# Layer-0 attention: the head norm's Newton steps on GpSimd, and the last 16 keys split on GpSimd from SBUF

## The chip, the cores and the metric

One Trainium2 chip, one core of it. The metric is device time in microseconds of one execution, the median of several runs. The profile is one further execution of the same program, with its own time. TensorE does matmuls and transposes, VectorE, ScalarE and GpSimd work on vectors; TensorE writes to PSUM, and GpSimd works from SBUF alone in this kernel.

## The reference, cut to what matters

An encoder of two layers over 1,040 positions (16 learned meta tokens and 1,024 tokens), width 1,024, all in float32. Layer 0 has two groups of heads. Group A is differential attention: four heads, each with two score maps that share one value matrix, and a norm over the head's output.

```python
def _diff_attention(q, k, v, lam, table, pos):
        ...
        s = jnp.einsum('bqhcd,bshcd->bhcqs', qb, k).astype(jnp.float32) * scale + bias[None, :, None]
        p = jax.nn.softmax(s, axis=-1)
        attn = p[:, :, 0] - lam * p[:, :, 1]
        return jnp.einsum('bhqs,bshv->bqhv', attn.astype(v.dtype), v)
...
    oa = _rmsnorm(oa, subln) * (1.0 - lam_init)
```

Group B is grouped-query attention (eight query heads, two key heads). Then come an output projection, a squared-ReLU MLP, and layer 1 with windowed attention and its own MLP.

## The kernel before

Each float32 operand of a product is split into a high part in the matmul's reduced format and a low part, the difference. A product is two or three matmuls over these parts. An attention weight is therefore transposed on TensorE into PSUM, copied to the high part by ScalarE (L570), and subtracted to the low part by VectorE (L572).

Part A, `head_a` (L603), runs over four heads. For each tile of 128 queries `scores` (L510) makes two maps in three chunks of 346 or 348 keys: matmuls (L519), eviction with the bias and a running minimum by VectorE (L521), the minimum of the three (L531), and the exponential with its row sum by ScalarE (L533). GpSimd then combines the two maps: it multiplies the second by its weight (L642) and adds it to the first (L643). The weight is the first map's sum times minus lambda, over the second map's sum: VectorE takes the reciprocal (L640), GpSimd the product (L641). The first map's own sum is not divided out, since the norm that follows removes it; the norm's epsilon is scaled by its square instead (L659).

Part B, `attend_b` (L685), runs over two key heads and four query heads of each, two query tiles at a time, and twice over the 16 remaining queries. It is the same with one map: VectorE evicts (L524), GpSimd divides (L694).

`pv` (L540) multiplies by the values. It is a generator. A group has two query tiles (in part A also one of two tiles and the 16 remaining queries). For each run of key blocks it transposes, splits and multiplies (L553, L570, L572, L584). The 1,040 keys are eight blocks of 128 and 16 more. For these 16 it transposes keys 912 to 1,039, takes the last 32 rows, and stacks them in one tile `tail`: high, low, and in part A high again, in steps of 32 partitions, against a value block laid out to match. Before the change this is the last step of the generator: ScalarE copies out of PSUM (L596), VectorE subtracts (L594), and the closing matmul (L597) follows. There are 16 such groups in part A and 34 in part B.

The generators wait in a list, `late`. After each group's scores the oldest is run, so that three stay open. The order of the instructions on each engine's queue is set by the framework's scheduler, which simulates the program with a cost table of its own. So the values of one group stand between the scores of later ones. Every queue runs in its order.

The head norm is `norm_a` (L654): ScalarE squares the head's output (L657), `colsum` (L181) sums it over partitions with 18 small matmuls (L187), evicts the sums (L197, L200) and calls `rsqrt_small` (L152). That one starts from a bit trick (L157, L158) and makes three Newton steps of three VectorE operations each (L160 to L162) on 128x9 elements. `norm_b`, placed behind up to two more groups, spreads the result over the partitions with another 18 matmuls (L210), and VectorE multiplies (L663). `rsqrt_small` also serves the other norms of the kernel.

Of the kernel before, what the change touches and what calls it, by code (L numbers as in the profile page):

```python
# [12 lines left out]
F32 = mybir.dt.float32  # L13
# [3 lines left out]
ALU = mybir.AluOpType  # L17
# [4 lines left out]
P = 128  # L22
L = 1040
# [4 lines left out]
EPS = 1e-6  # L28
# [40 lines left out]
def f32(ap):  # L69
    return ap.bitcast(F32)  # L70


def trunk(tc, hT, gT, w_in0, w_out0, w_up, w_down, w_in1, w_out1, rel, sinks, lamv, subln, qkn,
          onehot, ident_d, cos_d, sin_d, out, dbg=None, stop=None):
    nc = tc.nc
    V, A, G, T, D = nc.vector, nc.scalar, nc.gpsimd, nc.tensor, nc.sync
# [75 lines left out]
    def rsqrt_small(x, pw, n):  # L152

        y = sm.tile([P, 24], F32, tag="rs_y", bufs=2, name=nm("rsy"))
        t = sm.tile([P, 24], F32, tag="rs_t", bufs=2, name=nm("rst"))
        yv, tv = y[:pw, :n], t[:pw, :n]
        V.tensor_scalar(tv.bitcast(I32), x.bitcast(I32), 1, None, op0=ALU.arith_shift_right)  # L157
        V.tensor_scalar(yv.bitcast(I32), tv.bitcast(I32), -1, 0x5F3759DF, op0=ALU.mult, op1=ALU.add)  # L158
        for _ in range(3):
            V.tensor_tensor(tv, yv, yv, op=ALU.mult)  # L160
            V.scalar_tensor_tensor(tv, tv, -0.5, x, op0=ALU.mult, op1=ALU.mult)
            V.scalar_tensor_tensor(yv, tv, 1.5, yv, op0=ALU.add, op1=ALU.mult)  # L162
        return y
# [17 lines left out]
    def colsum(acc, c0, n, ps, scale, eps=None):  # L181
# [19 lines left out]
        return rsqrt_small(x[:, :nt], P, nt), tiles  # L201
# [338 lines left out]
    def pv(ps_o, ptiles, vmats, passes, lo_pool=()):  # L540
# [34 lines left out]
        slow = {r: split(r) for r in lo_pool}  # L575
        order = [r for r in range(len(runs)) if r not in slow] + list(lo_pool)
# [11 lines left out]
        pt, _ = transposed([L - P])  # L588
        tl = tails[tail_at[0] % 3]
        tail_at[0] += 1  # L590
        for x, (v, lo) in enumerate(passes):
            rows = slice(32 * x, 32 * x + 32)
            if lo:
                V.tensor_tensor(tl[rows, :gw], pt[96:128, :gw], f32(tl[0:32, :gw]), op=ALU.subtract)  # L594
            else:
                A.copy(tl[rows, :gw], pt[96:128, :gw])  # L596
# [6 lines left out]
    def head_a(h):  # L603
# [18 lines left out]
        for grp in GRPS:  # L622
            ptiles = []
            for t in grp:
# [16 lines left out]
                G.tensor_tensor(b[:, 1:2], es[:, t, 0:1], nlam, op=ALU.mult)  # L641
                G.tensor_scalar(st[1], st[1], b[:, 0:1], b[:, 1:2], op0=ALU.mult, op1=ALU.mult)  # L642
# [11 lines left out]
        def norm_a():  # L654
# [4 lines left out]
            V.scalar_tensor_tensor(e0, es[:, :, 0], EPS, es[:, :, 0], op0=ALU.mult, op1=ALU.mult)  # L659
            y, tiles = colsum(osq, 0, L, bank("tr"), 1.0 / 128, e0)  # L660
# [725 lines left out]
```

## Time and profile before

| | |
|---|---|
| median of 3 runs | 2,571.01 us (2,569.41 to 2,578.85) |
| profiled execution, its own time | 2,573.7 us |
| its span, first to last instruction | 2,571.9 us |
| mean granted clock of TensorE | 0.977 |
| TensorE, VectorE, ScalarE, GpSimd busy | 95%, 76%, 49%, 50% |

A row of the profile names line, engine, operation, what is written and read, and shapes. PE is TensorE's matmuls, PEld its weight loads, DVE VectorE, ACT ScalarE, POOL GpSimd, SP the queue that issues transfers. A busy TensorE isn't one at its peak: matmuls overlap, and the granted clock (1.00 is 2.4 GHz, 0.5 is 1.2 GHz) says how fast it ran. A wait is put down to the event that came last.

### The profile page before, as it was taken

To read this page: it belongs to the slowest core of one execution; us is meant where nothing else is said; L and a number is where in the kernel's file an instruction comes from. 1 tells how busy PE (TensorE), PEld (TensorE's weight loads), DVE (VectorE), ACT (ScalarE), POOL (GpSimd) and SP (SyncE) were. 2 spreads that over 40 slices of the span, in tenths; PEclk is the share of its full clock that TensorE was granted. 3 is DMA by queue.
4 is the path that set the end of the run, shared out by engine and by line. 5 is a ranking of instruction groups with operands and counts; after the bars stand their busy time and mean duration, and the time that the engine had idled before them with its cause. 6 is when DMAs were issued, how large, how long until landed. Compare 5 with 4: busy or idle time off the path is not lost. (4 is left out here: it accounts for less than half of the span.)

```text
span 2571.9 us, 43032 instructions
## 1 busy us (share of the span) xinstructions
PE 2448.4 (95%) x15375; PEld 2224.7 (86%) x15375; DVE 1947.2 (76%) x4059; ACT 1266.1 (49%) x2587; POOL 1283.1 (50%) x1221
## 2 busy tenths in 40 slices
PE   7999999999998999999999999998989999899997
PEld 7999888999998988989999998887878888677776
DVE  7843998899767677779898767787586665889975
ACT  3322766688634333354333447887344444443424
POOL 3300766233155555445666345556365664566645
PEclk9999998999998999999999999999989999999998
DMA  4287534100221733353433342232304334554411
GB/s 134 95 270 243 148 97 121 26 12 12 97 96 64 216 126 125 138 199 124 154 120 113 106 139 69 70 82 70 124 31 165 136 144 142 187 171 131 148 60 72
DMA packets 134614, 307.16 MB, mean 119 GB/s; under 512 B 18656, under 2 KB 49792, under 8 KB 133888
## 3 DMA queue, kind: packets, MB, share of 16 engines
q1 hardware_dynamic: 134400, 304.42, 36.3%
q8 instruction: 121, 1.98, 0.3%
q14 instruction: 93, 0.76, 0.1%
HBM read 214.43 MB, written 98.43 MB: 122 GB/s over the span
## 5 line engine op out<-in xcount | busy, mean ns | idle before, releaser
L876 PE MATMUL st<-h,wh 128*128 128x260 f32 (+1 forms) x2520 | 808.2, 325 | 41.1 <-DVE up L907 16.5
L876 PE MATMUL st<-l,wh 128*128 128x260 f32 (+1 forms) x2520 | 808.5, 323 | 7.7 <-DVE l L801 4.2
L876 PE MATMUL st<-h,wl 128*128 128x260 f32 (+1 forms) x2520 | 778.9, 323 | 6.0 <-DVE wl L133 4.0
L876 PEld LDWEIGHTS st<-h,wh 128*128 128x128 f32 x2520 | 478.1, 191 | 92.6 <-ACT up L908 15.4
L876 PEld LDWEIGHTS st<-l,wh 128*128 128x128 f32 x2520 | 480.7, 191 | 47.1 <-DVE l L996 5.2
L876 PEld LDWEIGHTS st<-h,wl 128*128 128x128 f32 x2520 | 472.6, 191 | 48.6 <-DVE wl L133 5.8
L132 ACT CAST wh<-wr 128x512 fp32r<-128x512 f32 x378 | 232.7, 617 | 420.4 <-PE st L876 197.9
L133 DVE TENSOR_TENSOR wl<-wr,wh 128x512 fp32r<-128x512 f32 x254 | 226.8, 897 | 159.5 <-ACT wh L132 159.0
L133 POOL TENSOR_TENSOR wl<-wr,wh 128x512 fp32r<-128x512 f32 x124 | 171.1, 1379 | 153.6 <-ACT wh L132 146.8
L908 ACT ACTIVATE up<-up 128x260 f32<-128x260 f32 (+1 forms) x192 | 93.5, 491 | 209.6 <-DVE up L907 209.2
L519 PE MATMUL sc<-stk,stk 128*128 128x346 f32 (+1 forms) x768 | 182.1, 353 | 11.8 <-DVE mx L521 11.6
L533 ACT ACTIVATE sp<-sp,mn 128x1040 f32<-128x1040 f32 x134 | 156.4, 1167 | 42.9 <-DVE mn L531 38.1
L996 DVE TENSOR_TENSOR l<-l,h 128x520 fp32r<-128x520 f32 (+1 forms) x182 | 172.7, 951 | 1.8 <-ACT h L994 1.8
L1027 DVE TENSOR_TENSOR h<-h,st 128x260 f32<-128x260 f32 x392 | 150.7, 415 | 28.1 <-PE st L876 26.5
L1027 DVE TENSOR_TENSOR hall<-hall,st 128x512 f32<-128x512 f32 x196 | 131.1, 679 | 28.3 <-PE st L876 27.0
L149 PE MATMUL mm<-l,wh 128*128 128x346 f32 (+3 forms) x440 | 151.1, 343 | 0.3 <-DVE l L784 0.3
L149 PE MATMUL mm<-h,wl 128*128 128x346 f32 (+3 forms) x440 | 149.9, 343 | 0.0
L886 POOL TENSOR_TENSOR ws<-wr 128x512 f32<-128x512 f32 x32 | 43.0, 1344 | 213.9 <-DMA wr<-w_up 191.4
L149 PE MATMUL mm<-h,wh 128*128 128x346 f32 (+3 forms) x440 | 148.3, 343 | 0.6 <-ACT h L783 0.6
L694 POOL TENSOR_SCALAR sp<-sp,rsum 128x1040 f32<-128x1040 f32 x66 | 75.4, 1155 | 144.9 <-DVE rsum L537 56.1
L907 DVE SCALAR_TENSOR_TENSOR up<-up,acc 128x260 f32<-128x260 f32 (+1 forms) x144 | 143.2, 997 | 5.5 <-ACT acc L219 2.1
L132 ACT CAST wh<-ws 128x512 fp32r<-128x512 f32 x120 | 74.3, 619 | 145.1 <-PE st L876 114.9
(286 smaller groups left out, 5980.1 us busy)
## 6 DMA issues: line engine op xcount, KB each, us to landing
wr<-w_down SPq DMA_DIRECT2D x68, 512.0 KB, 4.1
wr<-w_up SPq DMA_DIRECT2D x64, 512.0 KB, 4.1
l<-sd SPq DMA_DIRECT2D x42, 520.0 KB, 5.4
l<-sd SPq DMA_DIRECT2D x42, 512.0 KB, 4.9
stk<-stk_d SPq DMA_DIRECT2D x72, 260.0 KB, 6.5
sd<-up SPq DMA_DIRECT2D x30, 520.0 KB, 2.6
sd<-up SPq DMA_DIRECT2D x30, 512.0 KB, 2.6
wr<-w_in SPq DMA_DIRECT2D x27, 512.0 KB, 6.1
```

The lines of the kernel that those rows point to most:

```text
L132: A.copy(h, src)
L133: lo_on.tensor_tensor(l, src, f32(h), op=ALU.subtract)
L149: T.matmul(ps[:, :n], a[:, k % 4 * P:(k % 4 + 1) * P], x[k][:, o:o + n], start=(k == 0 and i == 0), stop=(k == len(xh) - 1 and i == 2))
L519: T.matmul(ps[:M, :n], q, k[:, o:o + n], start=(i == 0), stop=(i == len(ops) - 1))
L533: A.activation(s[:M, :L], s[:M, :L], AF.Exp, bias=mn[:M, x:x + 1], scale=-1.0, accum_out=sums[:M, x:x + 1])
L694: G.tensor_scalar(s, s, rs[:, i:i + 1], 1.0, op0=ALU.mult, op1=ALU.mult)
L876: T.matmul(acc_[x, o][:, :n], a[:, c], b[:, o:o + n], start=first and k == 0 and y == 0, stop=k == nk - 1 and y == 2, skip_group_check=not ...
L886: G.tensor_tensor(s1, a21, a22, op=ALU.add)
L907: V.scalar_tensor_tensor(r[:, c], src, 0.0, r_[:, c], op0=ALU.max, op1=ALU.mult)
L908: A.activation(r[:, c], r[:, c], AF.Square)
L996: V.tensor_tensor(l, src, f32(h), op=ALU.subtract)
L1027: marks.append(V.tensor_tensor(ht[m][:, c], ht[m][:, c], acc_[x, o][:, :n], op=ALU.add).ins)
```

## The change

Three edits, all in layer-0 attention.

1. In the head norm the three Newton steps run on GpSimd, as four operations each instead of three. The bit trick stays on VectorE. The scaled epsilon is made on GpSimd with two operations instead of one on VectorE. All other norms keep their code.
2. In `pv` the last keys are transposed first in the generator instead of last. ScalarE copies the 32 rows once into a new SBUF tile `traw` (two buffers), and GpSimd makes the parts of `tail` from it. The closing matmul stays last.
3. The weight of the second map is made by one VectorE operation behind the reciprocal, instead of one on GpSimd; the multiplication on GpSimd takes that one scalar.

```diff
-    def rsqrt_small(x, pw, n):
+    def rsqrt_small(x, pw, n, on=V):
...
         for _ in range(3):
-            V.tensor_tensor(tv, yv, yv, op=ALU.mult)
-            V.scalar_tensor_tensor(tv, tv, -0.5, x, op0=ALU.mult, op1=ALU.mult)
-            V.scalar_tensor_tensor(yv, tv, 1.5, yv, op0=ALU.add, op1=ALU.mult)
+            on.tensor_tensor(tv, yv, yv, op=ALU.mult)
+            if on is V:
+                V.scalar_tensor_tensor(tv, tv, -0.5, x, op0=ALU.mult, op1=ALU.mult)
+                V.scalar_tensor_tensor(yv, tv, 1.5, yv, op0=ALU.add, op1=ALU.mult)
+            else:
+                on.tensor_tensor(tv, tv, x, op=ALU.mult)
+                on.tensor_scalar(tv, tv, -0.5, 1.5, op0=ALU.mult, op1=ALU.add)
+                on.tensor_tensor(yv, yv, tv, op=ALU.mult)
...
         slow = {r: split(r) for r in lo_pool}
+        pt, _ = transposed([L - P])
+        tl = tails[tail_at[0] % 3]
+        tail_at[0] += 1
+        raw = getA("traw", [32, 272], F32, 2)
+        A.copy(raw[:, :gw], pt[96:128, :gw])
+        for x, (v, lo) in enumerate(passes):
+            rows = slice(32 * x, 32 * x + 32)
+            if lo:
+                G.tensor_tensor(tl[rows, :gw], raw[:, :gw], f32(tl[0:32, :gw]), op=ALU.subtract)
+            else:
+                G.tensor_copy(tl[rows, :gw], raw[:, :gw])
...
         yield
-        pt, _ = transposed([L - P])
-        tl = tails[tail_at[0] % 3]
-        tail_at[0] += 1
-        for x, (v, lo) in enumerate(passes):
-            rows = slice(32 * x, 32 * x + 32)
-            if lo:
-                V.tensor_tensor(tl[rows, :gw], pt[96:128, :gw], f32(tl[0:32, :gw]), op=ALU.subtract)
-            else:
-                A.copy(tl[rows, :gw], pt[96:128, :gw])
         T.matmul(ps_o[:, :gw], vmats[0][:, 8, :], tl[:, :gw], start=False, stop=True)
...
                 V.reciprocal(b[:, 0:1], es[:, t, 1:2])
-                G.tensor_tensor(b[:, 1:2], es[:, t, 0:1], nlam, op=ALU.mult)
-                G.tensor_scalar(st[1], st[1], b[:, 0:1], b[:, 1:2], op0=ALU.mult, op1=ALU.mult)
+                V.tensor_scalar(b[:, 1:2], b[:, 0:1], es[:, t, 0:1], nlam, op0=ALU.mult, op1=ALU.mult)
+                G.tensor_scalar(st[1], st[1], b[:, 1:2], 1.0, op0=ALU.mult, op1=ALU.mult)
...
-            V.scalar_tensor_tensor(e0, es[:, :, 0], EPS, es[:, :, 0], op0=ALU.mult, op1=ALU.mult)
-            y, tiles = colsum(osq, 0, L, bank("tr"), 1.0 / 128, e0)
+            G.tensor_scalar(e0, es[:, :, 0], EPS, 1.0, op0=ALU.mult, op1=ALU.mult)
+            G.tensor_tensor(e0, e0, es[:, :, 0], op=ALU.mult)
+            y, tiles = colsum(osq, 0, L, bank("tr"), 1.0 / 128, e0, G)
```

`colsum` hands its new argument `on` to `rsqrt_small`.

## Rows read from the trace of the kernel before

**Rows 1.** The page: span; busy time, share and instructions of each engine.

```profile
span 2571.9 us, 43032 instructions
...
PE 2448.4 (95%) x15375; PEld 2224.7 (86%) x15375; DVE 1947.2 (76%) x4059; ACT 1266.1 (49%) x2587; POOL 1283.1 (50%) x1221
```

**Rows 2.** Stretches: length; engines busy (instructions); granted clock; DMA share; GB/s.

```profile
316.00:331.00 15.00, 12.54 (x80) 11.41 (x80) 13.61 (x43) 7.79 (x15) 9.15 (x9) 0.89 0.00 1
331.00:367.00 36.00, 35.50 (x271) 34.50 (x269) 32.60 (x126) 28.28 (x58) 24.21 (x20) 1.00 0.64 167
367.00:391.00 24.00, 19.19 (x99) 15.60 (x98) 22.24 (x73) 11.61 (x22) 16.46 (x15) 0.86 0.26 60
425.00:442.00 17.00, 14.28 (x80) 12.74 (x80) 14.55 (x54) 8.20 (x16) 6.99 (x9) 0.80 0.17 42
477.00:492.00 15.00, 13.11 (x74) 12.50 (x75) 8.86 (x32) 5.15 (x11) 4.03 (x4) 0.66 0.01 2
500.00:660.00 160.00, 158.27 (x1210) 151.76 (x1209) 157.16 (x541) 136.50 (x258) 57.50 (x51) 1.00 0.05 12
255.00:450.00 195.00, 179.33 (x1199) 165.54 (x1198) 174.10 (x659) 133.62 (x264) 129.70 (x110) 0.94 0.45 121
```

**Rows 3.** Waits, 255 to 450 us: who for whom, us, times, longest.

```profile
PEld sc L519 <- DVE mx L521: 18.5, 27, 2.2
POOL sp L642 <- DVE mn L531: 15.9, 4, 5.0
...
PE sc L519 <- DVE mx L521: 11.6, 13, 1.9
```

**Rows 4.** Groups of VectorE, 255 to 495 us: busy us, mean ns; idle before.

```profile
L160 DVE TENSOR_TENSOR rst<-rsy 128x9 f32<-128x9 f32 x12 | 9.8, 818 | 0.2
L594 DVE TENSOR_TENSOR tail<-tr,tail 32x256 fp32r<-32x256 f32 (+2 forms) x17 | 7.2, 423 | 0.5
...
L659 DVE SCALAR_TENSOR_TENSOR e<-es 128x8 f32<-128x8 f32 x4 | 5.4, 1356 | 0.0
L640 DVE RECIPROCAL beta<-es 128x1 f32<-128x1 f32 x32 | 5.0, 157 | 2.7 <-ACT sp L533 2.7
...
L161 DVE SCALAR_TENSOR_TENSOR rst<-rst,cs 128x9 f32<-128x9 f32 x12 | 4.7, 390 | 0.0
...
L157 DVE TENSOR_SCALAR rst<-cs 128x9 int32<-128x9 int32 x4 | 2.5, 626 | 0.1
```

**Rows 5.** Timeline, first head's norm: start us, us, operation, [idle before].

```profile
317.25 2.42 POOL L643 TENSOR_TENSOR sp<-sp,sp 128x1040 f32<-128x1040 f32 x1
317.42 2.28 DVE L160 TENSOR_TENSOR rst<-rsy 128x9 f32<-128x9 f32 x1
...
320.19 0.59 PE L519 MATMUL sc<-stk,stk 128*128 128x348 f32 x2 [1.56 <-DVE mx L521]
```

**Rows 6.** Timeline, second head's norm.

```profile
367.52 2.43 POOL L643 TENSOR_TENSOR sp<-sp,sp 128x1040 f32<-128x1040 f32 x1
...
368.75 1.23 DVE L157 TENSOR_SCALAR rst<-cs 128x9 int32<-128x9 int32 x1
```

**Rows 7.** Groups of GpSimd, 255 to 450 us.

```profile
L642 POOL TENSOR_SCALAR sp<-sp,beta 128x1040 f32<-128x1040 f32 x32 | 39.0, 1220 | 43.9 <-DVE beta L640 25.1 <-DVE mn L531 15.9 <-PE sc L519 2.0
L641 POOL TENSOR_TENSOR beta<-es,nlam 128x1 f32<-128x1 f32 x32 | 6.2, 195 | 13.0 <-ACT sp L533 13.0
```

**Rows 8.** Line 649, ending a differential group: ns min/median/max, first and last start.

```profile
L649 ACT COPY oT<-pv x16: 352/372/393, 284.0 to 474.4; 128x256 f32<-128x256 f32 x12, 128x272 f32<-128x272 f32 x4
```

**Rows 9.** Groups of GpSimd behind layer-0 attention, 700 us to the end.

```profile
L1240 POOL TENSOR_SCALAR s<-s,rsum 128x400 f32<-128x400 f32 (+1 forms) x128 | 76.1, 608 | 43.3 <-DVE rsum L1238 42.3
...
L1269 POOL TENSOR_TENSOR oc<-oc,ob 64x256 f32<-64x256 f32 x40 | 29.7, 744 | 34.5 <-ACT oc L1268 33.0 <-issue 1.2
```

**Rows 10.** Groups, 500 to 660 us.

```profile
L584 PEld LDWEIGHTS pv<-plo,v 128*128 128x128 f32 x207 | 38.9, 188 | 8.0 <-DVE plo L572 6.1 <-DVE mn L531 0.7
...
L594 DVE TENSOR_TENSOR tail<-tr,tail 32x256 fp32r<-32x256 f32 (+1 forms) x26 | 11.0, 422 | 0.8
```

More of the change, by code (lines that the diff above doesn't have):

```diff
@@ L179, in sq_acc, with colsum @@
             add_on.tensor_tensor(acc[:, o:o + n], acc[:, o:o + n], t[:, :n], op=ALU.add)
-    def colsum(acc, c0, n, ps, scale, eps=None):
+    def colsum(acc, c0, n, ps, scale, eps=None, on=V):
         tiles = tok_tiles(c0, n)
@@ L200, in colsum @@
             V.tensor_scalar(x[:w, full:nt], src[:w, full:nt, 0], scale, EPS, op0=ALU.mult, op1=ALU.add)
-        return rsqrt_small(x[:, :nt], P, nt), tiles
+        return rsqrt_small(x[:, :nt], P, nt, on), tiles
     def bcast_cols(y, tiles, newps, use):
```

## The prediction

> **What bounds the kernel now.** I read the page first: TensorE is busy 95% of the span, VectorE 76%, GpSimd 50% [rows 1]. An average over unlike stages says little about an edit confined to one, so next comes the table of stretches of layer-0 attention. It has two parts. From 255 to about 450 us run the four differential heads (part A), from 500 to 700 the grouped-query heads (part B). In part A VectorE is busy 174.1 of 195 us, GpSimd 129.7 [rows 2]; in the steady stretch of part B VectorE is busy 157.2 of 160 us [rows 2]. VectorE is the engine to relieve in both.
>
> Four short stretches stand out: 316 to 331, 367 to 391, 425 to 442 and 477 to 492 us. They hold 80, 99, 80 and 74 matmuls, 333 in 71 us, or 4.7 per us, while the quiet stretch 331 to 367 holds 271 in 36 us, or 7.5 per us. The granted clock in them is 0.89, 0.86, 0.80 and 0.66 against 1.00 [rows 2]: part of the time TensorE ran at 1.2 instead of 2.4 GHz. Those four stretches are where the head norm of each of the four heads runs. The waits say who holds TensorE up: scores wait for VectorE's eviction (L521), 18.5 us at the weight loads and 11.6 us at the matmuls, 30.1 us in part A [rows 3].
>
> The group table of VectorE says why it is late. The Newton multiply of the reciprocal root (L160) works on 128x9 elements and takes 818 ns in the mean, the next one (L161; L162 has the same count, time and mean) 390, the small product for the epsilon (L659, 128x8) 1,356, the shift (L157) 626. A reciprocal on 128x1 (L640) takes 157 [rows 4]. The timeline shows the mechanism: GpSimd's add L643 starts at 317.25 and lasts 2.42 us; L160 starts at 317.42 and lasts 2.28, so both end at about 319.7. TensorE's next scores then start after an idle 1.56 us, put down to the eviction queued behind L160 [rows 5]. In the second norm the shift L157, started at 368.75, ends at 369.98 together with the L643 that ran from 367.52 [rows 6]. A tiny VectorE operation here waits out a whole GpSimd operation, and everything in VectorE's queue stands behind it. By the Trainium skill (SBUF — State Buffer, "Who interferes with whom") a VectorE instruction with two SBUF inputs cannot run beside a GpSimd instruction that reads SBUF, and one that has a single SBUF input and is in no two-port mode can; the pairs of rows agree, and so does L640, which never grew.
>
> **The change, part by part.**
>
> *Newton steps and epsilon product leave VectorE.* Per head nine Newton operations and L659 go. They held VectorE 9.8 + 4.7 + 4.7 + 5.4 = 24.6 us [rows 4]. At 157 ns each the forty would take 6.3 us, so 18.3 us of it is waiting for GpSimd. The shift and the subtraction that starts the guess stay, so the shift's waiting (2.5 us less 4 x 0.157, so 1.9) can stay too. What is this worth on the path? Lower bound 0: the column sums and the broadcast matmuls of the norm stay where they were and could keep the clock down by themselves. Upper bound: if all 333 matmuls of the four stretches ran at the quiet rate they would need 333 / 7.53 = 44.2 us, a gain of 26.8. I take 60%, 16 us, because the 18.3 us of waiting is the part with a known cause and because the first stretch shows the stall, not the norm's matmuls, ahead of the slow matmuls.
>
> On GpSimd the same work is twelve Newton and two epsilon operations per head, 56 in all. The nearest row is GpSimd's 128x1 multiply L641, 195 ns [rows 7]: 56 x 0.195 = 10.9 us of GpSimd time. The broadcast that needs the result is issued behind two more groups' values, and one group takes (474.4 - 284.0) / 15 = 12.7 us [rows 8], against 12 x 0.195 = 2.3 us plus at most two pairs of L642 and L643, 1.22 and 2.43 us each [rows 6, 7], 7.3 us. I take its delay at nothing; without that cover, a chain late by one L643 would cost 2.4 us a head, 10 us.
>
> *The last 16 keys' rows.* For each of 50 groups (16 in part A, 34 in part B) VectorE's subtraction L594 goes, 423 ns [rows 4]. ScalarE takes one copy out of PSUM instead of two (A) or one (B). GpSimd gets a subtraction and one or two copies of 32x256. Its nearest rows: a two-input operation on 64x256 takes 744 ns, a one-input one on 128x400 608 [rows 9]. For the copy, which no row shows at this width, the ends are 195 and 744 ns; between L641 and the 400-column row a line gives about 0.45 us, which I take. So 1.19 us a group in part B (40 us, with GpSimd busy 57.5 of 160 in its steady stretch [rows 2]) and 1.64 us in part A (26 us). The Trainium skill (GPSIMD Engine Reference, "Engine selection") says that two-input elementwise work is about twice as slow on GpSimd and belongs on VectorE; the rows agree, 744 against 423 ns, a factor of 1.76. By that rule the move would be a loss; by these rows it is one only where GpSimd has no room, which is the slower rival below.
>
> In part B one group takes 160 / 26 = 6.15 us by the count of L594, and the weight loads of the value products waited 8.0 us in those 160, 6.1 of it for VectorE's split [rows 10]. Scaled to the 200 us of part B that is 10 us at most, 0 at least (TensorE is itself busy 158.3 of 160 [rows 2]). I take half, 5 us. In part A 16 x 0.423 = 6.8 us leave VectorE.
>
> *The weight of the second softmax.* GpSimd loses L641 (32 x 195 ns = 6.2 us [rows 7]) and VectorE gains a scalar operation on 128x1, once per query tile. Its nearest row by size is L640, 157 ns: 32 x 0.157 = 5.0 us, against the 6.8 just saved in part A, so I take the two as cancelling. From the other side, L157 is the same operation on nine columns, 626 ns in the mean: 20 us. It also stands between the reciprocal and L642, which already waits 25.1 us for the reciprocal [rows 7]: about 0.16 us more for 32 tiles is 5 us of GpSimd waiting, with GpSimd three groups ahead of the values; I charge 2 us for this and for a fuller GpSimd. Its ends are 0 and those 5.
>
> *Sum.* -16 - 5 + 2 = -19 us. The profiled execution took 2,573.7 us (span 2,571.9), 2.7 above the median of the runs, 2,571.0; taken off the median, 2,552.
>
> **Rivals.**
>
> *GpSimd becomes the bound, and the tail comes late (slower).* GpSimd's 129.7 us of part A lose 6.2 and gain 26 and 11: 161 us in a stretch that should shrink from 195 to about 180, so 90% busy. The closing product L597 now needs GpSimd, in TensorE's fixed order. A tail taken at a group's start has 12.7 us [rows 8]; ahead of it in GpSimd's queue can stand two tiles (2 x 3.65 us) and the longest wait for a score, 5.0 us [rows 3], and with its own 1.64 that is 13.9. If each of 16 groups then waits for one L643, the price is 16 x 2.43 = 39 us, and the time 2,571 - 19 + 39 = 2,591. It decides from 19 / 16 = 1.2 us a group on. Against it: GpSimd's waits for inputs come to over 40 us in part A [rows 7], so it often had nothing to do. Chance 0.17.
>
> *The new scalar operation waits like L157.* Then VectorE gets 32 x (0.626 - 0.157) = 15 us back, and 2,571 - 19 + 15 = 2,567. For it: L157 is a scalar operation from SBUF to SBUF. Against it: L640, one column, never waited. Chance 0.09. The Trainium skill (VectorE: DVE Perf Modes, "What auto-detection actually checks") lets a one-source operation take the two-port mode where the outermost non-unit dimensions are even or equal; with one column there is none, so it leaves this open.
>
> *The clock stays down.* Column sums and broadcasts still run as 36 tiny matmuls a head, and the gain of the four stretches shrinks to their uncovered stall, some 2 us, with part B at 3: 2,566. For it: in the fourth stretch the clock was 0.66 though only part of its norm operations waited. Chance 0.14.
>
> *All of it comes.* 26.8 + 10 = 37 us: 2,534. Chance 0.10.
>
> **How the numbers follow.** Forecast 2,552 with chance 0.50, its own range 2,541 to 2,561 (8 to 24 us from the norm stretches, 0 to 8 from part B). The range for 8 in 10 reaches from 2,532, which takes in the largest gain, to 2,580, part of the way to the slower rival; it leaves out about 0.06 below and 0.13 above. A half per cent, 12.9 us, is about what a measurement here can tell from no change. Of the forecast's 0.50, 0.06 lies under that: faster 0.44 + 0.10 = 0.54; the same 0.06 + 0.09 + 0.14 = 0.29; slower 0.17.
>
> **What would show it.** Right: no VectorE operation on nine columns over 0.3 us except the shift; in the four norm stretches over 6 matmuls per us and a clock above 0.9; a part-B group near 6.0 us; no wait of L597 for GpSimd. Wrong: L597 or the pass after it waiting for the tail; the new scalar operation with a mean far above 157 ns; GpSimd busy throughout part A while TensorE idles; or norm stretches as slow as before with VectorE now free.

## The result, and the profile after

The changed kernel took 2,585.86 us (median of six runs, 2,583.55 to 2,586.71), the kernel before 2,570.97 beside it: a ratio of 1.0053, 95% interval 1.0041 to 1.0065. It is slower by 14.9 us; the forecast was 19 us faster. The profiled execution took 2,585.7 us, 12.0 more than the one of before.

The page's rows that answer to [rows 1]: VectorE lost 35 us and GpSimd gained 65, as the change says, but the span grew.

```profile
span 2583.6 us, 43002 instructions
...
PE 2450.2 (95%) x15375; PEld 2218.8 (86%) x15375; DVE 1912.6 (74%) x4001; ACT 1258.1 (49%) x2571; POOL 1348.2 (52%) x1361
```

Two starting times split the attention into its parts: the copy that ends the last differential group (L649 before, 474.4 us [rows 8]; now L656) and the last joined output of part B (L707 before, now L715). Below the first is called the end of A, and the difference of the two the length of B: 474.4 and 224.2 before. The row of before for L707, and then both of after:

```profile
L707 DVE TENSOR_TENSOR oc<-pv,ob x34: 273/406/417, 488.6 to 698.6; 64x256 f32<-64x256 f32 x32, 64x128 f32<-64x128 f32 x2
```

```profile
L656 ACT COPY oT<-pv x16: 349/374/404, 281.7 to 482.3; 128x256 f32<-128x256 f32 x12, 128x272 f32<-128x272 f32 x4
...
L715 DVE TENSOR_TENSOR oc<-pv,ob x34: 283/413/418, 494.3 to 709.8; 64x256 f32<-64x256 f32 x32, 64x128 f32<-64x128 f32 x2
```

So the end of A came 7.9 us later and B took 227.5, 3.3 more. What follows grew by 0.5 (2,583.6 - 709.8 against 2,571.9 - 698.6). That makes up the 11.7 us between the spans. Where A lost its time stands in the stretches of [rows 2]:

```profile
316.00:331.00 15.00, 14.30 (x99) 12.67 (x97) 13.52 (x55) 10.51 (x20) 14.84 (x12) 1.00 0.33 85
331.00:367.00 36.00, 27.82 (x151) 24.53 (x152) 21.09 (x85) 17.40 (x35) 26.81 (x32) 0.76 0.42 115
367.00:391.00 24.00, 24.00 (x187) 23.70 (x186) 20.66 (x86) 17.67 (x34) 17.16 (x20) 1.00 0.35 98
425.00:442.00 17.00, 17.00 (x121) 16.48 (x120) 14.05 (x60) 12.74 (x23) 11.79 (x12) 0.93 0.28 90
477.00:492.00 15.00, 14.38 (x95) 13.36 (x95) 11.53 (x43) 9.03 (x17) 9.03 (x16) 0.84 0.01 2
500.00:660.00 160.00, 155.55 (x1166) 145.83 (x1166) 142.47 (x493) 128.89 (x246) 80.57 (x98) 1.00 0.05 12
255.00:450.00 195.00, 178.28 (x1154) 161.62 (x1153) 154.10 (x645) 127.39 (x247) 146.98 (x150) 0.92 0.43 117
```

The first norm stretch now has 99 matmuls in place of 80, at full clock. But the quiet stretch behind it, 331 to 367, fell from 271 matmuls to 151 and from a granted clock of 1.00 to 0.76. VectorE is relieved: in part A its busy time fell from 174.1 to 154.1. GpSimd is busy 14.84 of the first 15 us. The timeline inside the bad stretch shows who holds whom:

```profile
335.55 2.39 POOL L650 TENSOR_TENSOR sp<-sp,sp 128x1040 f32<-128x1040 f32 x1
337.89 0.21 POOL L667 TENSOR_TENSOR e<-e,es 128x8 f32<-128x8 f32 x1
...
338.06 2.41 POOL L650 TENSOR_TENSOR sp<-sp,sp 128x1040 f32<-128x1040 f32 x1
...
338.56 1.46 PE L524 MATMUL sc<-stk,stk 128*128 128x348 f32 x6 [1.61 <-DVE mx L526]
...
340.42 0.21 POOL L167 TENSOR_TENSOR rsy<-rsy,rst 128x9 f32<-128x9 f32 x1
340.50 0.52 DVE L526 CUSTOM_DVE_ANT_0 sp<-sc,toe 128x348 f32<-128x348 f32 x1 [0.94 <-POOL sp L650]
...
341.70 0.21 POOL L160 TENSOR_TENSOR rst<-rsy 128x9 f32<-128x9 f32 x1
...
341.86 2.40 POOL L650 TENSOR_TENSOR sp<-sp,sp 128x1040 f32<-128x1040 f32 x1
...
344.23 0.20 POOL L165 TENSOR_TENSOR rst<-rst,cs 128x9 f32<-128x9 f32 x1
...
350.00 4.15 PE L215 MATMUL tr<-ident,rsy 128*128 128x128 f32 x18
```

GpSimd makes one Newton step of 0.2 us (L160, L165 to L167), then mostly one or two whole multiplies or adds of 1.1 and 2.4 us (L649 and L650, which are L642 and L643 of before), then the next step. VectorE's eviction L526 waits until L650 gives a score buffer back, and TensorE's scores wait for the eviction. From its first step at 326.00 to its last at 349.17 the chain of twelve operations, 2.4 us of work, takes 23.4 us. The four heads' chains take 23.4, 12.8, 15.1 and 3.9 us, 55 in all.

What the long chain does to TensorE stands in TensorE's order. The broadcast L215 begins at 350.00, right behind the chain's last step. The last transpose or value product of a run of keys ahead of it ended at 329.5, and the next transpose starts at 354.56. For 20.5 us TensorE had nothing but scores and one closing product, while the scores' evictions wait for GpSimd to free their buffers. Over the four heads such gaps come to 35.2 us, for 14.9 before the change (0.5 in the first head).

The waits of 255 to 450 us answer to [rows 3]: the scores' waits for evictions, 30.1 us before, are 34.6. They are put down to VectorE, the last event; VectorE's own waits there for a score buffer come to 6.8.

```profile
POOL sp L649 <- DVE beta L648: 22.0, 7, 10.5
PEld sc L524 <- DVE mx L526: 21.5, 32, 2.8
...
PE sc L524 <- DVE mx L526: 13.1, 8, 2.5
...
DVE sp L526 <- POOL sp L650: 6.8, 7, 2.2
```

The groups of 255 to 505 us price the single operations; first VectorE's, then GpSimd's.

```profile
L648 DVE TENSOR_SCALAR beta<-beta,es,nlam 128x1 f32<-128x1 f32 x32 | 8.7, 271 | 0.4
...
L647 DVE RECIPROCAL beta<-es 128x1 f32<-128x1 f32 x32 | 5.1, 159 | 14.9 <-ACT sp L538 14.9
...
L157 DVE TENSOR_SCALAR rst<-cs 128x9 int32<-128x9 int32 x4 | 2.5, 634 | 0.1
```

```profile
L589 POOL TENSOR_TENSOR tail<-traw,tail 32x256 fp32r<-32x256 f32 (+2 forms) x19 | 13.8, 725 | 1.5
L591 POOL CAST tail<-traw 32x256 fp32r<-32x256 f32 (+2 forms) x35 | 13.7, 392 | 31.9 <-ACT traw L585 30.9
...
L160 POOL TENSOR_TENSOR rst<-rsy 128x9 f32<-128x9 f32 x12 | 2.4, 203 | 1.2 <-DVE rsy L158 0.6
```

### The profile page after: what moved, and what is told of

Same layout as the page of the kernel before. It is cut to its first block, busy times and chain, and to the rows that moved or that the text cites. A ratio compares the mean times of both kernels' runs of the same rounds, so it can differ in the third digit from the quotient of the medians.

```text
span 2583.6 us, 43002 instructions
## 1 busy us (share of the span) xinstructions
PE 2450.2 (95%) x15375; PEld 2218.8 (86%) x15375; DVE 1912.6 (74%) x4001; ACT 1258.1 (49%) x2571; POOL 1348.2 (52%) x1361
## 5 line engine op out<-in xcount | busy, mean ns | idle before, releaser
L1004 DVE TENSOR_TENSOR l<-l,h 128x520 fp32r<-128x520 f32 (+1 forms) x182 | 166.6, 917 | 1.7 <-ACT h L1002 1.7
L1035 DVE TENSOR_TENSOR hall<-hall,st 128x512 f32<-128x512 f32 x196 | 131.4, 680 | 29.2 <-PE st L884 27.3
L524 PEld LDWEIGHTS sc<-stk,stk 128*128 128x128 f32 x768 | 123.5, 198 | 31.9 <-DVE mx L526 21.5
L577 DVE TENSOR_TENSOR plo<-tr,ph 128x512 fp32r<-128x512 f32 (+1 forms) x212 | 134.0, 647 | 22.7 <-ACT ph L575 22.1
```

The source lines that it names most:

```text
L524: T.matmul(ps[:M, :n], q, k[:, o:o + n], start=(i == 0), stop=(i == len(ops) - 1))
L577: V.tensor_tensor(plo[:, :w], pt[:, :w], f32(ph[:, :w]), op=ALU.subtract)
L1004: V.tensor_tensor(l, src, f32(h), op=ALU.subtract)
L1035: marks.append(V.tensor_tensor(ht[m][:, c], ht[m][:, c], acc_[x, o][:, :n], op=ALU.add).ins)
```

## The experiments

The runs were timed in five groups, each beside the kernel before on one chip (2,570 to 2,572.5 us). The first theory was that GpSimd's total load is what costs, with the keys' work as its largest part; the first rival, that it is the Newton chain threaded between GpSimd's large operations. "Keys first" and "keys last" are the place of the last 16 keys in `pv`; "old engines" are ScalarE's copy and VectorE's subtraction out of PSUM. The table holds the medians, the ratio to before with its interval, the end of A and length of B in the profile, and the sum of the four Newton chains where they run on GpSimd. The end of A and B come from one profiled execution each. Executions of one kernel spread by 3 to 14 us, and the profiled one of the kernel before took 2.7 us more than the median; one to three us in these two columns decide nothing.

| kernel | us | ratio | end of A | B | chains |
|---|---|---|---|---|---|
| before | 2,571.0 | | 474.4 | 224.2 | |
| the change | 2,585.9 | 1.0053 (1.0041, 1.0065) | 482.3 | 227.5 | 55.1 |
| 1 Newton on GpSimd alone | 2,564.0 | 0.9975 (0.9965, 0.9984) | 464.6 | 223.9 | 29.2 |
| 2 keys first, on GpSimd, alone | 2,584.7 | 1.0052 (1.0035, 1.0068) | 475.6 | 228.6 | |
| 3 keys first, old engines | 2,591.2 | 1.0080 (1.0063, 1.0098) | 474.1 | 236.4 | |
| 4 Newton on VectorE out of PSUM | 2,566.0 | 0.9981 (0.9972, 0.9991) | 467.3 | 223.2 | |
| 5 softmax weight alone | 2,570.0 | 0.9990 (0.9981, 1.0000) | 471.9 | 224.2 | |
| 6 keys last, on GpSimd | 2,569.1 | 0.9988 (0.9978, 0.9998) | 476.6 | 215.0 | |
| 7 the change without softmax weight | 2,594.8 | 1.0081 (1.0062, 1.0101) | 491.8 | 227.3 | 66.2 |
| 8 keys ahead of the last run, old engines | 2,567.4 | 0.9983 (0.9973, 0.9994) | 470.9 | 220.9 | |
| 9 = 1 and 6 | 2,591.8 | 1.0074 (1.0051, 1.0096) | 501.0 | 213.9 | 60.7 |
| 10 = 1 and 3 | 2,592.3 | 1.0071 (1.0046, 1.0097) | 478.9 | 234.2 | 46.8 |
| 11 = 1, and 6 in part B only | 2,554.0 | 0.9925 (0.9908, 0.9942) | 462.8 | 215.1 | 29.7 |
| 12 = 11 and 5 | 2,557.9 | 0.9938 (0.9921, 0.9955) | 464.6 | 215.2 | 29.1 |
| 13 keys ahead of the second run, old engines | 2,580.9 | 1.0031 (1.0018, 1.0043) | 477.0 | 225.7 | |
| 14 = 3, in B out of the output's bank | 2,566.2 | 0.9978 (0.9969, 0.9987) | 476.4 | 215.8 | |
| 15 = 11, in A keys ahead of the last run | 2,568.5 | 0.9987 (0.9978, 0.9997) | 476.5 | 214.1 | 54.4 |
| 16 = 4 and 6 | 2,567.0 | 0.9980 (0.9971, 0.9990) | 474.0 | 215.3 | |
| 17 = 15 with the Newton steps of 4 | 2,555.2 | 0.9942 (0.9929, 0.9955) | 462.4 | 213.7 | |
| 18 = 3 and 4 | 2,584.6 | 1.0053 (1.0038, 1.0069) | 473.0 | 233.8 | |

### Runs 1 to 4: the parts

Run 1 (the epsilon product goes with it, as in the change):

```diff
-            V.tensor_tensor(tv, yv, yv, op=ALU.mult)
...
+            on.tensor_tensor(tv, yv, yv, op=ALU.mult)
...
-            y, tiles = colsum(osq, 0, L, bank("tr"), 1.0 / 128, e0)
+            y, tiles = colsum(osq, 0, L, bank("tr"), 1.0 / 128, e0, G)
```

> The head norm's Newton steps and its epsilon product on GpSimd, all else as before. Theory (GpSimd's throughput is what part A now runs at, and the tails are its largest new load, 26 us against 11): this part alone is harmless or a gain, 2,550 to 2,568 us, and the four norm stretches hold over 6 matmuls per us. Rival (the chain of twelve Newton steps is threaded one by one between GpSimd's large operations, takes some 20 us a head, and the broadcast and all that stands behind it in TensorE's order wait for it): this part alone is slower, 2,578 to 2,590 us, and the chain from its first to its last step takes over 15 us.

Run 2 makes the edit of `pv` alone:

```diff
+        raw = getA("traw", [32, 272], F32, 2)
+        A.copy(raw[:, :gw], pt[96:128, :gw])
...
+                G.tensor_tensor(tl[rows, :gw], raw[:, :gw], f32(tl[0:32, :gw]), op=ALU.subtract)
+            else:
+                G.tensor_copy(tl[rows, :gw], raw[:, :gw])
```

> The tails taken first and split on GpSimd, all else as before. Theory (throughput of GpSimd): most of the loss is here, 2,580 to 2,592 us. Rival (the Newton chain): near or below the kernel before, 2,562 to 2,573 us.

Run 3 moves the block of the keys, unchanged, to the head of the generator:

```diff
         slow = {r: split(r) for r in lo_pool}
+        pt, _ = transposed([L - P])
...
         yield
-        pt, _ = transposed([L - P])
```

> The tails taken first, but copied by ScalarE and subtracted by VectorE out of PSUM as before: the place is changed, not the engine. If the tail's engine is what costs: as before, 2,566 to 2,575 us. If the new place in the order costs (a bank of PSUM taken early, another interleaving with the scores): slower like the run with GpSimd, over 2,578 us.

Run 4 leaves the Newton steps on VectorE, with one operand in the free part of the sums' PSUM bank, so that no step reads two operands from SBUF; three small copies and one small multiply a head are added.

```diff
+            V.tensor_copy(yv, yp)
+            V.tensor_tensor(tv, yv, yp, op=ALU.mult)
+            V.tensor_tensor(tv, tv, xp, op=ALU.mult)
+            V.scalar_tensor_tensor(yv if i == 2 else yp, tv, 1.5, yp, op0=ALU.add, op1=ALU.mult)
```

> The Newton steps stay on VectorE, but the guess and the sums lie in PSUM, so that no step has two SBUF inputs or both ends in SBUF; three small copies are added per head, and the epsilon product stays as before. If small VectorE operations with two SBUF inputs wait for GpSimd, no step takes over 0.3 us here, and the norm stretches speed up: 2,550 to 2,565 us. If they waited for something else, the means stay near 0.4 to 0.8 us and the time near 2,571 us.

The Newton steps alone gain 6 us (end of A 9.8 earlier), and they gain 4 us without GpSimd (run 4, 1 us above its band): its groups of VectorE, 255 to 505 us, show steps that wait for nobody.

```profile
L676 DVE SCALAR_TENSOR_TENSOR e<-es 128x8 f32<-128x8 f32 x4 | 3.2, 793 | 0.1
...
L176 DVE TENSOR_TENSOR rst<-rst,tr 128x9 f32<-128x9 f32 x12 | 1.9, 162 | 0.2
L175 DVE TENSOR_TENSOR rst<-rsy,tr 128x9 f32<-128x9 f32 x12 | 1.9, 162 | 0.1
```

The multiply that took 818 ns [rows 4] takes 162; the epsilon product, both of whose inputs stayed in SBUF, still takes 793. The rule of the Trainium skill that the prediction drew on (SBUF — State Buffer, "Who interferes with whom") says this of an instruction with at most one SBUF input, outside the two-port modes, and the trace agrees.

The keys' edit loses 14 us by itself, and run 3 shows where: the place alone loses 21, all of it in and behind part B, and the other engines give some 6.5 back. In 560 to 620 us run 3 made 417 matmuls; the row of the kernel before stands first:

```profile
560.00:620.00 60.00, 59.54 (x454) 56.54 (x453) 58.45 (x200) 50.33 (x96) 21.41 (x19) 1.00 0.05 12
560.00:620.00 60.00, 57.80 (x417) 51.90 (x415) 55.60 (x184) 45.67 (x88) 19.46 (x18) 1.00 0.05 11
```

Its waits of 500 to 660 us show ScalarE waiting for transposes (17.6 us, 7.0 before) and TensorE waiting for splits, 18.3 us at weight loads and matmuls, where [rows 10] had 6.1 at the weight loads:

```profile
ACT ph L570 <- PE tr L553: 17.6, 16, 2.0
PEld pv L593 <- DVE plo L572: 13.6, 37, 0.5
...
PE pv L593 <- DVE plo L572: 4.7, 16, 0.3
```

GpSimd's load can't be what costs in part B, since run 3 puts none of the keys' work there. That half of the first theory fell here.

### Runs 5 to 8: the rest of the sum, and the place

Run 5 is the third edit of the change alone (its diff stands above), run 7 the whole change without it. Run 6 keeps the keys last and only changes their engines, as run 2 does. Run 8 takes the old block one step earlier:

```diff
         for r in order:
             yield
+            if r == order[-1]:
+                pt, _ = transposed([L - P])
...
             ph, plo = slow[r] if r in slow else split(r)
```

> The softmax-weight edit alone: the product that forms the second softmax's weight moves from GpSimd to VectorE, behind the reciprocal. In the changed kernel this VectorE operation took 271 ns, 32 times, 8.7 us of VectorE in part A, and GpSimd loses 32 x 0.195 = 6.2 us. Theory (the extra 7 us that the parts don't explain, +15 measured against -6 for the Newton steps and +14 for the last keys, come from GpSimd being loaded by both at once): this edit alone moves little, 2,566 to 2,574. Rival (it is this edit that costs them, since TensorE's scores wait for what stands in VectorE's queue): 2,575 to 2,582.

> The whole change without its softmax-weight edit: Newton steps and epsilon product on GpSimd, the last 16 keys first and split on GpSimd. Theory (the two loads on GpSimd get in each other's way: the Newton chain of the first head took 23 us with both against 12 with the Newton steps alone): 2,582 to 2,588, as slow as the whole change or a little slower, since GpSimd keeps 6 us more; chain of the first head about 20 us. Rival (the parts add up and the softmax-weight edit costs the rest): 2,575 to 2,580, the sum 2,570 - 6 + 14.

> The last 16 keys are split by GpSimd from a ScalarE copy, as in the change, but they stay in their old place, after the last run of a group; nothing else is changed. Theory (the place costs some 21 us, the move between engines gives back some 7: the two numbers of the runs with the tail first, 2,591 and 2,585): 2,558 to 2,568. Rival (the engine move only pays where the tail comes early; in the last place the closing product waits for a chain of a ScalarE copy of 0.37 us, a GpSimd copy of 0.39 and a GpSimd subtraction of 0.73, 1.5 us for each of 50 groups, part of it covered): 2,578 to 2,610, with a wait of the closing product for GpSimd in the trace.

> The last 16 keys are taken one step earlier than in the kernel before, just ahead of a group's last run instead of behind it, with the engines of before. Theory (the tail costs at the head of a group because its transposes, its bank and its copies stand ahead of the first run's split, which value products then wait for; one step early it stands ahead of the last run alone): between the ends, 2,568 to 2,580, with TensorE's waits for VectorE's split between 6.8 and 21.8 us in 500 to 690. Rival (any change of the written order costs, because the rows' order on every engine is planned from it anew): 2,582 to 2,595.

The softmax weight's edit moves the end of A by -2.5 us alone and by -9.5 beside the other two (482.3 against 491.8): it is the only edit that takes work off GpSimd. So it doesn't cost the missing microseconds. By the ends of A the edits apart make -9.8 + 1.2 - 2.5 = -11.1, together +7.9: 19 us from their meeting. By the medians of the times they make -6.1 + 14.6 - 2.5 = +6.0 apart and +14.9 together, so the meeting costs some 9 us; that the profiles say more is in part the one of before, 2.7 us above its median, which the three parts count three times and the change once. Run 7 missed both its bands (2,594.8; the upper one ended at 2,588). It differs from run 2 by the Newton edit alone: the edit that gains 6 us by itself costs 8 to 10 beside the keys (A from 475.6 to 491.8).

Run 6 missed its band by 1 us (2,569.1 for 2,558 to 2,568) but shows the engine's worth in part B plainly: 215.0 for 224.2 us. TensorE is busy in all of 60 us there:

```profile
560.00:620.00 60.00, 60.00 (x482) 59.55 (x481) 57.24 (x203) 52.72 (x101) 34.29 (x42) 1.00 0.05 12
```

Its rival, a closing product late by GpSimd, did not come. Run 8 is a little faster than before, just below its band, and TensorE waited less for splits (2.4 us in 500 to 690) than the 6.8 to 21.8 expected: not any new order costs.

### Runs 9 to 12: what meets on GpSimd, and a faster kernel

Run 9 joins runs 1 and 6, run 10 runs 1 and 3. Run 11 is run 1 with the keys last and, in part B only, on GpSimd; run 12 adds the softmax weight's edit.

```diff
+        pool_ = len(passes) == 2
+        src = pt[96:128, :gw]
+        if pool_:
+            src = getA("traw", [32, 272], F32, 2)[:, :gw]
+            A.copy(src, pt[96:128, :gw])
...
+                (G if pool_ else V).tensor_tensor(tl[rows, :gw], src, f32(tl[0:32, :gw]), op=ALU.subtract)
```

> Newton steps and epsilon product on GpSimd, and the last 16 keys split on GpSimd in their old, last place, in both parts of the attention. By the copy that ends part A (474.4 us before) and the last joined output of part B (224.2 us later before), the runs so far split the edits: Newton alone -9.8 in A, keys first with the old engines +12.2 in B, GpSimd instead of ScalarE and VectorE -9.2 in B, Newton with keys first on GpSimd +17.4 in A. Theory (in A the Newton chain and the keys' work get in each other's way on GpSimd, wherever the keys stand): the end of A at 480 or later, B about 215, time 2,565 to 2,580. Rival (it is the first place that gets in the way of the norm, through the banks of PSUM that both take, not GpSimd's load): the end of A at 462 to 472, B about 215, time 2,550 to 2,560.

> Newton steps and epsilon product on GpSimd, and the last 16 keys taken first, but still copied by ScalarE and subtracted by VectorE out of PSUM. GpSimd has no work of the keys here. Theory (GpSimd's load): the end of A at 462 to 470 as with the Newton steps alone, B 234 to 238, time 2,575 to 2,585. Rival (the first place and the norm hinder each other): the end of A at 480 or later, time above 2,590.

> Newton steps and epsilon product on GpSimd; the last 16 keys stay in their old place, and only in part B, where GpSimd does not carry the heads' Newton steps, they go through a ScalarE copy and GpSimd. Theory (parts that do not meet on GpSimd add up): the end of A at 465 (-9.8), B 215 (-9.2), time 2,549 to 2,557. Rival (what is won in one part is given back in the next, since part B starts out of another state and the planned order differs): 2,560 to 2,568.

> The kernel of the run before with the softmax-weight edit added (one product of 271 ns on VectorE in place of one of 195 ns on GpSimd per query tile, 32 tiles). Alone this edit moved the end of A by -2.5 us, and beside the full load on GpSimd by -9.5. Theory (it helps as far as GpSimd is loaded; with the Newton steps alone there it is worth the small end): 2,546 to 2,556, 0 to 4 us below the run before. Rival (on VectorE the 8.7 us stand ahead of the evictions that scores wait for, once VectorE has lost the Newton steps' waits): 2 to 9 us above the run before.

In run 9 each half is worth something alone, and together A ends at 501.0, 26.6 us late; its time, 2,591.8, lies above both bands. Its waits of 255 to 505 us hold, once, the one that the prediction's slower rival named, the closing product for the keys' part on GpSimd:

```profile
PEld pv L604 <- POOL tail L601: 7.0, 1, 7.0
...
PE pv L604 <- POOL tail L601: 6.7, 1, 6.7
```

Run 10's end of A came out between its branches, at 478.9, and its time in the rival's: GpSimd carries none of the keys, yet the chains take 46.8 us. So the keys' load is not needed for the harm; a changed order is enough to thread the chain between large operations. Run 11 beats both kernels: 0.9925. Its stretches show both parts better, 1,275 matmuls for 1,199 and 1,258 for 1,210 [rows 2]:

```profile
255.00:450.00 195.00, 182.09 (x1275) 171.12 (x1273) 164.54 (x673) 143.54 (x287) 142.90 (x155) 0.96 0.46 125
500.00:660.00 160.00, 158.97 (x1258) 157.87 (x1257) 150.97 (x499) 140.18 (x263) 87.69 (x105) 1.00 0.11 36
```

In part A GpSimd has the same work in runs 10 and 11 (busy 138.4 and 142.9 us of 255 to 450, same view), and yet run 10 ends A 16 us later: it is not the total that decides, and the rest of the first theory fell with it. The softmax weight's edit adds 3.9 us to run 11 rather than taking any off, in its rival's branch, though the two intervals overlap.

### Runs 13 to 16: the bank, and the chain

Run 13 is run 8 with `order[1]` for `order[-1]`. Run 14 is run 3, but in part B the keys are transposed into the free half of the group's output bank:

```diff
+        if len(passes) == 2:
+            pt, off = ps_o[:, 256:512], 0
+            for p, cw, sel in ptiles:
+                T.transpose(pt[:, off:off + cw], p[:, L - P:L], ident)
+                off += cw
+        else:
+            pt, _ = transposed([L - P])
```

Run 15 is run 11 with the keys of part A placed as in run 8; run 16 joins runs 4 and 6.

> The last 16 keys are taken ahead of a group's second run, with the engines of before. In part B (last copy of A to last joined output) the first place took 236.4 us, ahead of the last run 220.9, the last place 224.2. Theory (the tail hurts because at the head of a group its transposes, bank and copies stand ahead of the first split, when TensorE has no other value products of that group): part B 220 to 228 us, time 2,566 to 2,576, as good as the later places. Rival (the earlier the worse, step by step, since the tail's copies hold up every run behind them): part B 229 to 234, time 2,577 to 2,586.

> As the run with the keys first and the old engines (2,591 us; part B 236.4), but in part B the keys are transposed into the free upper half of the group's own output bank, not into a bank of the ring that the runs' transposes use. Theory (the tail's copies stand ahead of the first run's on ScalarE and VectorE, whatever bank they come from): part B 232 to 238, time 2,586 to 2,593. Rival (it is the bank taken out of the ring of three that delays the runs): part B 215 to 226, time 2,569 to 2,580.

> The fastest kernel so far (Newton steps on GpSimd; keys through GpSimd in part B alone, in the last place; 2,554 us, end of A 462.8) with the keys of part A one step earlier, ahead of a group's last run, on the old engines; alone, that place moved the end of A by -3.5 us. Theory (parts that do not share an engine's queue add up): end of A 459 to 464, time 2,549 to 2,555. Rival (an earlier place and the Newton steps hinder each other, as the keys first did, end of A 478.9): end of A 470 or later, time 2,560 to 2,570.

> Newton steps on VectorE with their operands in PSUM (end of A 467.3 alone), the keys through ScalarE and GpSimd in the last place in both parts (end of A 476.6, B 215.0 alone). With the Newton steps on GpSimd instead, the end of A was 501.0 and the time 2,592. Theory (the chain of small operations on GpSimd, threaded between the keys' operations and the large ones, is what is late, and with it the norm and the last keys): end of A 466 to 478, B about 215, time 2,556 to 2,568. Rival (GpSimd with the keys is too full for a faster norm in any form): end of A 485 or later, time above 2,572.

Run 14 settles part B against the theory stated for it. Same place, same engines, same operations; with the bank taken out of the ring of three that the runs' transposes use, B takes 215.8 us in place of 236.4, less than before the change (the time, 2,566.2, is 3 us below the rival's band):

```profile
560.00:620.00 60.00, 60.00 (x472) 58.10 (x471) 59.35 (x206) 52.11 (x99) 21.41 (x19) 1.00 0.05 13
```

Its waits of 500 to 660 us halve those of run 3 at the transposes and quarter those for the split; before the change they were 7.0 and 6.4 us:

```profile
ACT ph L570 <- PE tr L553: 8.9, 14, 0.9
...
PEld pv L599 <- DVE plo L572: 4.8, 20, 0.3
```

VectorE is no less busy than before (59.35 of 60 us for 58.45), and TensorE makes 472 matmuls for 454. So VectorE's load did not limit part B in the kernel before. That the ring limited it there too fits, but isn't shown: run 14 differs from before in the place as well as the bank, and keys last out of the output's bank weren't tried. Run 13's B, 225.7, is nearly that of the last place, so in B the harm belongs to the head of the group and doesn't fade step by step; its time, 2,580.9, lies in the rival's band and is 5 us worse than A and B explain.

Run 15 fell to its rival: the end of A 476.5, with a chain of 31.2 us in the second head. Run 16 takes the chain off GpSimd and leaves the keys there: A ends at 474.0, 27 us earlier than run 9's.

### Runs 17 and 18: is the long chain a cause or a companion?

Runs 15 and 10 again, with the Newton steps as in run 4.

> The kernel with the keys of part A ahead of a group's last run and those of part B through GpSimd (end of A 476.5, four Newton chains 54 us on GpSimd, time 2,568), with the Newton steps on VectorE and their operands in PSUM. Theory (the long chain on GpSimd makes A late): end of A 462 to 470, time 2,550 to 2,560. Rival (the earlier place of the keys makes A late whenever the norm is faster, and the chain is long because of that): end of A 474 or later, time 2,563 to 2,572.

> The kernel with the keys first on the old engines and the Newton steps on GpSimd (end of A 478.9, four chains 47 us, part B 234.2, time 2,592), with the Newton steps on VectorE and their operands in PSUM instead. Theory (the chain): end of A 464 to 472, B 234 to 237, time 2,578 to 2,586. Rival (the place): end of A 476 or later, time 2,588 to 2,596.

Run 17: the end of A goes from 476.5 to 462.4, the time to 2,555.2, level with run 11. Run 18: from 478.9 to 473.0, time 2,584.6 as the theory had it, though A ends 1 us outside its band. In both orders A recovers as soon as the chain leaves GpSimd, by 14.1 and 5.9 us. TensorE's order shows what the chain held up. Second head, run 15 and then run 17: the last closing product, the broadcast behind the chain, and the next transposes.

```profile
371.63 0.28 PE L615 MATMUL pv<-tail,v 128*128 128x256 f32 x1
...
395.38 2.10 PE L524 MATMUL sc<-stk,stk 128*128 128x348 f32 x6 [6.49 <-DVE mx L526]
397.28 3.79 PE L215 MATMUL tr<-ident,rsy 128*128 128x128 f32 x18
...
402.07 1.47 PE L558 MATMUL tr<-ident,sp 128*128 128x128 f32 x12
```

```profile
373.94 0.28 PE L627 MATMUL pv<-tail,v 128*128 128x256 f32 x1
...
376.19 2.27 PE L227 MATMUL tr<-ident,rsy 128*128 128x128 f32 x18
...
379.45 1.47 PE L570 MATMUL tr<-ident,sp 128*128 128x128 f32 x12
```

In run 15 TensorE had only scores for 25.5 us ahead of the broadcast, in run 17 for 2.1; in the first head of runs 10 and 18 it was 15.4 and 1.1. The profile puts next to none of this down to the chain (0.2 us in run 15), because what stands behind the broadcast does not wait for an event: it isn't its turn. The long chain is a cause. In run 18 some 6 us (473.0 against run 4's 467.3) stay with the place. The change itself with its Newton steps off GpSimd wasn't run.

Where no large operation comes between, step follows step (run 1, third head, timeline). Ten of the twelve steps took 2.8 us there; a multiply and an add came ahead of the last two, and the whole chain took 7.6:

```profile
423.27 0.21 POOL L160 TENSOR_TENSOR rst<-rsy 128x9 f32<-128x9 f32 x1
...
423.57 0.21 POOL L165 TENSOR_TENSOR rst<-rst,cs 128x9 f32<-128x9 f32 x1
423.87 0.20 POOL L166 TENSOR_SCALAR rst<-rst 128x9 f32<-128x9 f32 x1
424.16 0.21 POOL L167 TENSOR_TENSOR rsy<-rsy,rst 128x9 f32<-128x9 f32 x1
```

## Why the prediction was wrong

**The step that failed: the last keys were costed as work that changes engines, not as a bank that changes place.** The prediction gave the edit -5 us in part B and no term for its new place. Alone it measured +14.6 by the medians, a miss of 20 us, the largest of the three terms (the Newton steps -6.1 for -16, the softmax weight -2.5 for +2). In the change B grew by 3.3. In B the place costs 10 to 12 us in three pairs (236.4, 234.2 and 233.8 against 224.2, 223.9 and 223.2; runs 3, 10, 18 against before, 1, 4). The engines give back 7.8 where the keys are first (run 2 against 3) and 9.2 where they are last (run 6). Run 14 shows that at the head of a group the place costs through the shared ring of banks. That the engines help for the same reason, one ScalarE copy of 0.37 us giving the bank back instead of a copy and a subtraction, fits but is only argued.

**The reading behind it.** "VectorE is the engine to relieve in both" was taken from 157.2 busy us of 160 [rows 2]. In part B it was false: run 14 relieves no engine and gains 8.4 us there, nearly as much as run 6. A row in view, TensorE waiting 8.0 us [rows 10], was put down to VectorE, the last event; that a bank let the split start late in the kernel before is likely, but only argued.

**The Newton steps: right in sign, too large, and then undone.** Alone they moved the end of A by -9.8 and the time by -6, not -16; how the rest of the 26.8 us of the upper bound is shared between the clock and the norm's own matmuls wasn't taken apart. In the change they were worth nothing, because "I take its delay at nothing" fell, the second step that failed. The sum of 2.3 us for the twelve steps plus at most two pairs of large operations, 7.3, assumed that the steps follow each other. They took 3.9 to 23.4 us a head, mostly with one or two large operations between links. The cover was also smaller than the two groups of 12.7 us that it was set against: in every head of the kernel before and of the change, at most one group closes between the column sums and the broadcast, and the values of later groups come behind it. The price named for the lost cover, one add a head or 10 us in all, had the right kind and was too small: by the profiles, the edits apart would have ended A at 463.3 (474.4 - 11.1), and it ended at 482.3.

**The slower rival.** It forecast 2,591 through GpSimd, and the time was 2,586, but by another wait; that the numbers lie close is luck. In the change the closing product (now L604) never waited for GpSimd. GpSimd held up the score buffers and the norm instead. Its own wait came in run 9, where the keys stand last. "90% busy" was 147.0 of 195 us, 75%; the local number, 14.84 of 15, is the one that mattered.

**What held.** No VectorE operation of the Newton steps is left; the shift still waits (634 ns); GpSimd's copy and subtraction took 392 and 725 ns, for 450 and 744; a Newton step 203 ns, for 195. The new softmax operation took 271 ns, not 157, so 8.7 us for 5.0, and was never held by GpSimd: that rival didn't come. One sign of being right came true and misled: the four norm stretches hold 6.3 to 7.8 matmuls per us, since the norms came later and lie only in part in these fixed windows.

**A slip in the sum.** The forecast's own range ends at 2,561; its terms at their small ends, 8 and 0 us gained and 2 charged, give 2,565. The measured time lies far outside both.

**What stays open.** Why one written order gives a chain of 3 us and another one of 31, and why no later group's values go ahead of the broadcast, lies in the order that was planned, which the trace shows but doesn't explain. Every edit has that order planned anew, so no run changes one thing alone. Between runs 9 and 16 the keys and the chain on GpSimd cost 27 us together, and how much of this is the late closing product wasn't taken apart. Runs 3, 6, 7 and 13 spent 4 to 6.5 us more than the kernel before behind part B (span less the start of the last joined output), in code that the edits don't touch; for this I have no cause.

## What to carry to other kernels

When a step is moved within a group, write down what it holds (a bank, a buffer) and which ring that comes from, and cost the place by itself: here it was worth more than the change of engine, with the opposite sign. A chain of tiny dependent operations costs on a shared engine not its own 2.4 us but whatever the order puts between its links, and TensorE pays for it through what stands behind the chain's result in its order, which the list of waits doesn't show. Give the chain an engine with short operations; here operands in PSUM made VectorE one (162 ns a step). And an engine that is busy 98% of a stretch is not its limit until something shows that relieving it moves the end.

## What the runs showed of the hardware

- A VectorE scalar operation on one column with two scalars from SBUF took 265 to 275 ns in 32 instances, at least 13 of them beside a GpSimd operation of over 1 us, and was never held up by one. The reciprocal of the same size took 159, and the nine-column scalar operation from SBUF to SBUF, L157, 634 in the mean.
- With one operand in PSUM the nine-column operations took 148 to 172 ns in all 48 instances of run 4, 29 of them beside a GpSimd operation of about 1 us or more. The Trainium skill (GPSIMD Engine Reference, "Engine selection") would leave two-input work on VectorE; per operation the rows agree (725 ns against 423), but in part B the slower engine gained 9.2 us, so the operation's length wasn't what bound there.
- Part B of every kernel with the keys off the ring, or on it for one copy in the last place, took 213.7 to 215.8 us, with TensorE busy 60.00 of 60 and 472 to 482 matmuls: that looks like its floor in this form.
